# A hybrid encoder block: q and k of both halves projected before V, all turned by VectorE

## The chip, the cores and the metric

The kernel runs on one core of a Trainium2 chip. The metric is device time of one execution in microseconds (us). The kernel before takes 1110.05 us (median of 3 runs, 1109.37 to 1110.4). Engines are named as in the profile: PE (TensorE's matmuls), PEld (its weight loads), DVE (VectorE), ACT (ScalarE), POOL (GpSimd), SP (SyncE, here only a queue that issues transfers).

## The reference

One layer on x of 512 tokens by 1024 features, all in float32: a half-step feed-forward block, then a mixer with two branches, then a second half-step feed-forward block. The tokens are an 8 x 64 grid; attention looks at a window of 8 rows by 16 columns.

```python
x = x + 0.5 * swiglu_1(rmsnorm(x))
h = rmsnorm(x)
xr, gr, q, k, v, ga, gb = split(h @ w_in)          # 7 parts of 1024 columns
xc = dwconv4(xr)                                   # then forward and backward RG-LRU
y_lru = (rglru_fwd(xc) + rglru_bwd(xc)) * gelu(gr)
q = rmsnorm_per_head(q) * 64 ** -0.5               # 16 heads of 64
k = rmsnorm_per_head(k)
s = q . k over the 8 x 16 window + bias[head, drow, dcol]
y_att = softmax(s) @ v
x = x + (sigmoid(ga) * y_lru + sigmoid(gb) * y_att) @ w_out
x = x + 0.5 * swiglu_2(rmsnorm(x))
```

## The kernel before

Every matmul is made of three passes: each float32 operand is split into a high and a low part (ACT writes the high part, line 145, DVE the low one, line 148), and PE adds high x low, high x high and low x high. A weight tile of 128x1024 (512 KB) comes by SP's queue into `wraw` (3 buffers) and is split into `wh` and `wl` (4 buffers each); PE uses such a tile, a chunk here, for 24 matmuls of 512 columns.

The stage that matters runs from about 358 to 700 us. First come eight chunks for the LRU's x (`wxr`), then the projections of q, k and V, each in two halves of 512 columns (8 heads). One half of one projection is a group: four chunks, four PSUM tiles `acc` by tokens (`tok_group`, lines 834 to 836). Then come 24 chunks of gates (`wg`), and the output projection.

Beside these groups the rest of the mixer is woven in by hand. It is written as Python generators, the lanes: `lru`, `att`, `tail`, `v` and `prep`. After each piece of PE work `weave` lets every lane go on by as many steps as the table RATE gives for the present phase (the phases here: xr, t0, t1, g). The program so written is then ordered for each engine by a scheduler: an engine's instructions, and the transfers that SP issues, run strictly in the order that comes out, and each waits for what it needs. `hold` ties an instruction behind PE's last projection matmul.

The groups come in the order q, k, V of the first half, then q, k, V of the second. q and k (`qk_raw`) are evicted by ACT to `qk` tiles with tokens on the partitions (line 846), squared and summed. They have to be normed and turned so that features lie on the partitions:

- First half: `norm_qk` scales them (line 912), and in `heads`, tile by tile (four feature tiles of two heads each), `start` has PE turn them against an identity, 4 + 4 matmuls of 128x128 (lines 949 and 951), into auxiliary PSUM. From there ACT and DVE make the high and low parts `qh`, `ql`, `kh`, `kl`.
- Second half: DVE turns them in blocks of 32x32 (line 916), SP stores them to DRAM (`qd`), and `fetch` brings one feature tile back, in pieces of 256 bytes, into `xqk` (one buffer), the next tile when `start` has read the last.

V is evicted by DVE (line 859), stored to DRAM by SP (`vd`, line 863) and read back by POOL in shifted forms (`vs`, `va`, `ve`).

Attention then goes in units. `scores` is 12 matmuls (line 988) per unit in the first half (8 units), 24 in the second (4 units); DVE adds the bias and takes the maximum (line 1008), ACT exponentiates and scales (lines 1015 and 1020); `ship` turns the weights on DVE (lines 1029 and 1030), stores them by SP (`pd`) and reads them back by POOL into `PT`. `apply` multiplies them by V (line 1051), ATT_LAG units later.

The lane `lru` does the gated recurrence by LRU_PLAN: small gate matmuls on PE (line 742), ACT's functions, DVE's scans (lines 787 and 789).

Of the kernel before, what the change touches and what calls it, by code (L numbers as in the profile page):

```python
# [9 lines left out]
F32 = mybir.dt.float32  # L10
# [6 lines left out]
P = 128  # L17
T = 512
# [45 lines left out]
ATT_LAG = 4, 2  # L64
# [20 lines left out]
    "t0": {"att": 0.0, "lru": 3.25},  # L85
    "t1": {"att": 0.75, "tail": 0.75, "lru": 2, "prep": 1.0},
    "g": {"att": 0.7, "tail": 0.7, "lru": 1.5, "v": 0.5, "prep": 1.0},
# [4 lines left out]
def block_kernel(ctx: ExitStack, tc, a, out):  # L92
# [616 lines left out]
    def lru():  # L709
# [17 lines left out]
        def cut(f):  # L727
            cuts[f] = tuple(big.tile([P, T], F32R, tag="PT", bufs=5, name=nm(n)) for n in ("ch", "cl"))
            split(xc[f], *cuts[f])
# [32 lines left out]
        def use(f, d):  # L762
            r, ix = got[f, d]
            hold(nc.vector.tensor_tensor(ix, ix, xc[f], ALU.mult))
            if d == 1 and f < 3:
                th = big.tile([P, T], F32, name=nm("th"), **(dict(tag="xqk", bufs=1) if f == 0 else dict(tag="PT", bufs=5)))
            else:
                th = big_t(n="th")
            act("tanh", nc.scalar.activation(th, r, AF.Tanh, scale=sp4[:, f * 2 + d : f * 2 + d + 1]))
            got[f, d] = r, ix, th  # L770
# [128 lines left out]
    def norm_qk(raws, st, qd):  # L899

        rq = tiny.tile([P, 2, NCB, 8], F32, tag="rq", name=nm("rq"))
        for w in range(2):
            for j in range(NCB):
                hold(nc.vector.tensor_scalar(rq[:, w, j, :], st[:, w, j, :], 1.0 / HD, epsv[:, j : j + 1],
                                             ALU.mult, ALU.add))
        hold(nc.scalar.activation(rq, rq, AF.Sqrt))
        nc.vector.reciprocal(rq, rq)
        yield
        for j in range(NCB):
            for w in range(2):  # L910
                t = raws[w][j].rearrange("p (h d) -> p h d", d=HD)
                hold(nc.vector.tensor_tensor(t, t, rq[:, w, j, :].unsqueeze(2).to_broadcast([P, 8, HD]), ALU.mult))
            if qd is not None:
                t2 = pair_t().rearrange("p a b -> p (a b)")
                for w in range(2):
                    nc.vector.transpose(
                        t2.rearrange("p (c f w i) -> p w f c i", c=NCB, f=4, w=2)[:, w],
                        raws[w][j].rearrange("p (f c i) -> p f c i", c=NCB, i=32))
                nc.sync.dma_start(qd[j], t2)
                yield  # L920
            elif j % 2 == 1:
                yield
        if qd is not None:
            yield
            fetch(qd, 0)

    xs = {}

    def fetch(qd, fi):
        t = xs[fi] = big.tile([P, NCB * NCB, 2, 32], F32, tag="xqk", bufs=1, name=nm("xqk"))  # L930
        for c in range(NCB):
            nc.sync.dma_start(
                t[c * 32 : (c + 1) * 32].rearrange("p g w i -> p g (w i)"),
                qd.rearrange("j (a i) c f x -> c f i (j a) x", a=NCB)[c, fi])

    def heads(hf, raws, qd):

        if hf == 1:
            until("prep", lambda: False)
# [3 lines left out]
        def start(fi):  # L943
            rev = lambda t: t.rearrange("p (j t) -> p j t", j=NCB)[:, :, ::-1]
            if hf == 0:
                fs = slice(fi * P, (fi + 1) * P)
                pq, pk = aux_t(), aux_t()
                for j in range(NCB):
                    hold(nc.tensor.transpose(pq[:, j * P : (j + 1) * P], raws[0][j][:, fs], ident))
                for j in range(NCB):  # L950
                    hold(nc.tensor.transpose(perm(pk)[:, j], raws[1][j][:, fs], ident))
                xq, xk = pq.rearrange("p (j t) -> p j t", j=NCB), pk
                q_of, k_of = rev, lambda t: t
            else:
                x = xs.pop(fi).rearrange("p (j a) w i -> p w j a i", j=NCB)
                xq, xk = x[:, 0], x[:, 1].rearrange("p j a (r c) -> p j a r c", r=2)
                q_of = lambda t: rev(t).rearrange("p j (a i) -> p j a i", i=32)
                k_of = lambda t: t.rearrange("p (a r j c) -> p j a r c", a=NCB, r=2, j=NCB)
# [7 lines left out]
            if hf == 1 and fi < 3:  # L966
                fetch(qd, fi + 1)
# [55 lines left out]
        def ship(fi, n2):  # L1023
# [9 lines left out]
            PT = big.tile([P, NCB, 7, 32], F32, tag="PT", bufs=5, name=nm("PT"))  # L1033
# [65 lines left out]
    bias(0)  # L1099
    for hf in range(2):  # L1100
        st = tiny.tile([P, 2, NCB, 8], F32, tag="st", name=nm("st"))
        raws = [qk_raw(0, hf, st), qk_raw(1, hf, st)]
        if hf == 1:
            qd = dram.tile([NCB, P, NCB, 4, 64], F32, name="qd")
            lanes["prep"].append(norm_qk(raws, st, qd))
        v_get(hf)
        if hf == 0:
            lanes["att"].append(norm_qk(raws, st, None))
        lanes["att"].append(heads(hf, raws, qd if hf == 1 else None))
        phase[0] = "t1" if hf == 0 else "g"  # L1110

# [145 lines left out]
```

## Time and profile before

| | |
|---|---|
| median of 3 runs | 1110.05 us |
| the profiled execution, in whole | 1108.49 us |
| its span on the core | 1106.7 us |
| PE busy in the span | 1093.7 us, 99% |
| granted PE clock | 1.0 throughout |
| bytes moved | 180 MB, 163 GB/s on average |

A page counts an engine as busy from an instruction's start to its end. PE's matmuls are pipelined and overlap, so what a matmul costs in a row of equal ones is the distance of the starts, not its duration. The views that the prediction uses are the busy time of each engine in stretches of 50 us, the groups of instructions by line and tile, the waits (who waited, for what, how long in total, how often, longest), the chain of work that ended last in order of time, and single instructions in order of time. Times in them count from the start of the span.

### The profile page before, as it was taken

The numbers are of one execution on the slowest core, as the hardware profiler recorded it, in microseconds if no ns is written. First come the engines' busy times: TensorE is split into PE (matmuls) and PEld (weight loads), VectorE is DVE, ScalarE is ACT, GpSimd is POOL, SyncE is SP. The second block draws the span as 40 slices with busy tenths as digits, with TensorE's granted clock in tenths as the row PEclk, the third lists the DMA queues.
The fourth block names the chain that finished last, engine by engine and source line by source line (L and its number), as shares of the span: only waits on it lengthen the run. The fifth ranks groups of instructions, "written<-read, shape, count | busy, mean of one in ns | idle before, by whom it ended". The sixth has DMA issues, their size and how long they took to land.

```text
span 1106.7 us, 17673 instructions
## 1 busy us (share of the span) xinstructions
PE 1093.7 (99%) x6779; PEld 969.0 (88%) x6779; DVE 796.1 (72%) x1228; ACT 619.1 (56%) x950; POOL 140.1 (13%) x243
## 2 busy tenths in 40 slices
PE   9999999999999999999999899999999999999998
PEld 7899999988888778787877778889999999998887
DVE  7877777795745786998886664659877777784642
ACT  8554544464443668777778673456655454464430
POOL 0000000000000342231325430001000000000000
PEclk9999999999999999999999999999999999999999
DMA  8576656643423576573799973477665666653421
GB/s 268 153 172 153 148 158 160 165 153 96 134 81 105 163 231 172 157 225 111 222 281 256 270 219 97 131 227 163 184 164 149 165 166 146 151 167 96 133 76 39
DMA packets 68452, 180.02 MB, mean 163 GB/s; under 512 B 17681, under 2 KB 21265, under 8 KB 68369
## 3 DMA queue, kind: packets, MB, share of 16 engines
q1 hardware_dynamic: 52160, 131.94, 36.8%
q0 software_dynamic: 15632, 46.70, 21.5%
q8 instruction: 53, 0.87, 0.3%
q10 hardware_dynamic: 576, 0.26, 0.1%
q14 instruction: 31, 0.25, 0.1%
HBM read 152.63 MB, written 17.83 MB: 154 GB/s over the span
## 4 chain that ended last, share of the span: by engine, by line
PE 95%; DMA 1%; DVE 1%; ACT 1%; issue 1%; SPq 0%; ACTq 0%; DVEq 0%
PE acc L312 31%; PE acc L172 11%; PE acc L173 10%; PE acc L174 10%; PE aux L312 5%; PE acc L834 4%; PE aux L172 4%; PE aux L174 4%; PE aux L173 4%; PE acc L835 4%; PE acc L836 4%; PE aux L1051 1%; PE aux L742 1%; PE aux L988 1%; DMA vd<-v 1%
## 5 line engine op out<-in xcount | busy, mean ns | idle before, releaser
L145 ACT ACTIVATE wh<-wraw 128x1024 fp32r<-128x1024 f32 (+3 forms) x236 | 233.4, 991 | 321.6 <-issue 90.5
L148 DVE TENSOR_TENSOR wl<-wraw,wh 128x1024 fp32r<-128x1024 f32 (+3 forms) x236 | 267.6, 1137 | 99.5 <-ACT wh L145 95.9
L312 PE MATMUL acc<-s,wh 128*128 128x256 f32 x1280 | 232.2, 283 | 0.0
L312 PEld LDWEIGHTS acc<-s,wh 128*128 128x128 f32 x1280 | 199.7, 192 | 0.0
L312 PE MATMUL acc<-s,wl 128*128 128x256 f32 x640 | 181.2, 283 | 0.0
L312 PEld LDWEIGHTS acc<-s,wl 128*128 128x128 f32 x640 | 122.9, 192 | 0.0
L172 PE MATMUL acc<-xh,wh 128*128 128x512 f32 x272 | 107.7, 396 | 0.0
L174 PE MATMUL acc<-xh,wl 128*128 128x512 f32 x272 | 106.3, 391 | 0.0
L173 PE MATMUL acc<-xl,wh 128*128 128x512 f32 x272 | 106.0, 390 | 0.0
L312 PE MATMUL acc<-xl,wh 128*128 128x256 f32 x320 | 90.6, 283 | 0.0
L312 PE MATMUL acc<-xh,wl 128*128 128x256 f32 x320 | 90.6, 283 | 0.0
L312 PE MATMUL acc<-xh,wh 128*128 128x256 f32 x320 | 90.6, 283 | 0.0
L834 PE MATMUL acc<-wh,xh 128*128 128x512 f32 x192 | 75.7, 394 | 1.0 <-ACT qk L846 1.0
L148 DVE TENSOR_TENSOR hl<-h,hh 128x512 fp32r<-128x512 f32 x88 | 57.3, 687 | 25.4 <-PE aux L173 24.2
L835 PE MATMUL acc<-wh,xl 128*128 128x512 f32 x192 | 74.8, 390 | 0.0
L836 PE MATMUL acc<-wl,xh 128*128 128x512 f32 x192 | 74.8, 389 | 0.0
L172 PE MATMUL aux<-hh,wh 128*128 128x512 f32 (+1 forms) x181 | 69.9, 386 | 0.0
L173 PE MATMUL aux<-hl,wh 128*128 128x512 f32 (+1 forms) x181 | 69.9, 386 | 0.0
L174 PE MATMUL aux<-hh,wl 128*128 128x512 f32 (+1 forms) x181 | 69.9, 386 | 0.0
L174 PE MATMUL acc<-hh,wl 128*128 128x512 f32 (+1 forms) x176 | 68.0, 386 | 0.0
L173 PE MATMUL acc<-hl,wh 128*128 128x512 f32 (+1 forms) x176 | 68.0, 386 | 0.0
L172 PE MATMUL acc<-hh,wh 128*128 128x512 f32 (+1 forms) x176 | 67.9, 386 | 0.0
(226 smaller groups left out, 2281.8 us busy)
## 6 DMA issues: line engine op xcount, KB each, us to landing
wraw<-wqkv SPq DMA_DIRECT2D x24, 512.0 KB
wraw<-wg SPq DMA_DIRECT2D x24, 512.0 KB
wraw<-w1d SPq DMA_DIRECT2D x22, 512.0 KB
wraw<-w2s SPq DMA_DIRECT2D x22, 512.0 KB
pair<-w2s SPq DMA_DIRECT2D x22, 512.0 KB
wraw<-w2d SPq DMA_DIRECT2D x22, 512.0 KB
wraw<-w1s SPq DMA_DIRECT2D x18, 512.0 KB
pair<-w1s SPq DMA_DIRECT2D x18, 512.0 KB
```

The costliest lines, as they stand in the source:

```text
L145: nc.scalar.activation(H, raw, AF.Copy)
L148: return nc.vector.tensor_tensor(L, raw, H.bitcast(F32), ALU.subtract)
L172: nc.tensor.matmul(ps, wh, xh, start=first, stop=False, skip_group_check=skip)
L173: nc.tensor.matmul(ps, wh, xl, start=False, stop=False, skip_group_check=skip)
L174: mark["mm"] = nc.tensor.matmul(ps, wl, xh, start=False, stop=last, skip_group_check=skip)
L312: mm = nc.tensor.matmul(o, w_[:, c], x_, start=first and m + k == 0 and w_ is H and x_ is xh_, stop=m + k == 4 and w_ is L, skip_group_che ...
L742: prev, mm = mm, nc.tensor.matmul(ps[d][b], W[w][o, c], X[x][o], start=x == 1, stop=w + x == 0)
L834: nc.tensor.matmul(pss[j], xh[kk][:, tj], H[:, s], start=kk == 0, stop=False)
L835: nc.tensor.matmul(pss[j], xl[kk][:, tj], H[:, s], start=False, stop=False)
L836: mark["mm"] = nc.tensor.matmul(pss[j], xh[kk][:, tj], L[:, s], start=False, stop=kk == KT - 1)
L988: mm = hold(nc.tensor.matmul(ps[hp][:, cs], q_[o, n * P : (n + 1) * P], keys(k_[o]), start=k_ is kl, stop=q_ is ql))
L1051: mm = nc.tensor.matmul(pv[h2 * HD : (h2 + 1) * HD, n * P : (n + 1) * P], vt[:, (fi * 2 + h2) * HD : (fi * 2 + h2 + 1) * HD], PT[:, q], st ...
```

## The change

The order of the six groups becomes q, k of the first half, q, k of the second, V of the first, V of the second. `norm_qk` now turns both halves by DVE into a `qd` of its own for each half, in the lane `prep`, while the next group runs; `heads` no longer uses PE for it. `xqk` has two buffers, and two tiles are fetched ahead: tiles 0 and 1 by `norm_qk`, tiles 2 and 3 when `start` has read the tile two before. The fetches of the second half wait until tile 3 of the first half has been asked for. PT has 4 buffers instead of 5, and the LRU's `th` tiles use the two `xqk` buffers and PT. RATE has one more phase (t2), fewer LRU steps per call in most phases, and no attention before t2; the first half's value product comes 3 units after its scores instead of 4.

```diff
-ATT_LAG = 4, 2
+ATT_LAG = 3, 2
...
-    "t0": {"att": 0.0, "lru": 3.25},
-    "t1": {"att": 0.75, "tail": 0.75, "lru": 2, "prep": 1.0},
-    "g": {"att": 0.7, "tail": 0.7, "lru": 1.5, "v": 0.5, "prep": 1.0},
+    "t0": {"att": 0.0, "lru": 3},
+    "t1": {"att": 0.0, "lru": 2.5, "prep": 1.25},
+    "t2": {"att": 0.7, "tail": 0.7, "lru": 2, "prep": 1.0},
+    "g": {"att": 0.6, "tail": 0.6, "lru": 1.5, "v": 0.5, "prep": 1.0},
...
-            if d == 1 and f < 3:
-                th = big.tile([P, T], F32, name=nm("th"), **(dict(tag="xqk", bufs=1) if f == 0 else dict(tag="PT", bufs=5)))
+            if d == 1 and f < 4:
+                th = big.tile([P, T], F32, name=nm("th"), **(dict(tag="xqk", bufs=2) if f < 2 else dict(tag="PT", bufs=4)))
...
-    def norm_qk(raws, st, qd):
+    def norm_qk(hf, raws, st):
...
         for j in range(NCB):
+            t2 = pair_t().rearrange("p a b -> p (a b)")
             for w in range(2):
                 t = raws[w][j].rearrange("p (h d) -> p h d", d=HD)
                 hold(nc.vector.tensor_tensor(t, t, rq[:, w, j, :].unsqueeze(2).to_broadcast([P, 8, HD]), ALU.mult))
-            if qd is not None:
...
+                nc.vector.transpose(
+                    t2.rearrange("p (c f w i) -> p w f c i", c=NCB, f=4, w=2)[:, w],
+                    raws[w][j].rearrange("p (f c i) -> p f c i", c=NCB, i=32))
+            nc.sync.dma_start(qd[hf][j], t2)
             yield
-            fetch(qd, 0)
+        while hf == 1 and (0, 3) not in xs:
+            yield
+        for fi in range(2):
+            fetch(hf, fi)
...
-            if hf == 0:
-                fs = slice(fi * P, (fi + 1) * P)
-                pq, pk = aux_t(), aux_t()
-                for j in range(NCB):
-                    hold(nc.tensor.transpose(pq[:, j * P : (j + 1) * P], raws[0][j][:, fs], ident))
-                for j in range(NCB):
-                    hold(nc.tensor.transpose(perm(pk)[:, j], raws[1][j][:, fs], ident))
...
+            x = xs[hf, fi].rearrange("p (j a) w i -> p w j a i", j=NCB)
...
-            if hf == 1 and fi < 3:
-                fetch(qd, fi + 1)
+            if fi < 2:
+                fetch(hf, fi + 2)
...
+    def qk_half(hf):
+        st = tiny.tile([P, 2, NCB, 8], F32, tag="st", name=nm("st"))
+        raws = [qk_raw(0, hf, st)]
+        if hf == 1:
+            phase[0] = "t2"
+        raws.append(qk_raw(1, hf, st))
+        qd[hf] = dram.tile([NCB, P, NCB, 4, 64], F32, name=nm("qd"))
+        lanes["prep"].append(norm_qk(hf, raws, st))
+        lanes["att"].append(heads(hf))
+
     for hf in range(2):
...
+        qk_half(hf)
+        phase[0] = ("t1", "t2")[hf]
+    for hf in range(2):
         v_get(hf)
...
+    phase[0] = "g"
```

Three places of the order that the scheduler makes. The first is PE's, at the first tile of the first half: before, in the third chunk of the second half's k group, `aux` taking the turned `qk` tiles.

```order
L836 MATMUL acc_5123<-wl_5159,xh_3092 128x512
...
L836 MATMUL acc_5123<-wl_5159,xh_3094 128x512
L949 MATMUL aux_5187<-ident,qk_4441 128x128
L949 MATMUL aux_5187<-ident,qk_4443 128x128
L949 MATMUL aux_5187<-ident,qk_4445 128x128
L949 MATMUL aux_5187<-ident,qk_4447 128x128
L951 MATMUL aux_5188<-ident,qk_4626 128x8x16
L951 MATMUL aux_5188<-ident,qk_4628 128x8x16
L951 MATMUL aux_5188<-ident,qk_4630 128x8x16
L951 MATMUL aux_5188<-ident,qk_4632 128x8x16
L834 MATMUL acc_5120<-wh_5208,xh_3096 128x512
```

The same place now, after the same number of rows on PE: the middle of the first half's V group (lines are one higher in this part, ten lower further down).

```order
L836 MATMUL acc_5122<-wh_5182,xl_3095 128x512
L837 MATMUL acc_5122<-wl_5183,xh_3094 128x512
L978 MATMUL aux_5213<-kl_5156,qh_5153 128x256
L978 MATMUL aux_5212<-kl_5156,qh_5153 128x256
L978 MATMUL aux_5213<-kh_5155,qh_5153 128x256
L978 MATMUL aux_5212<-kh_5155,qh_5153 128x256
```

The turns are gone, and the scores of the first unit stand at this point; the next unit's follow two chunks later, at the end of the group.

The second place is SP's queue around the stores of the first half's V (`vd`). Before, weights of the next group (`wraw_5124`, `wraw_5157`) are asked for ahead of these stores; the loads of the second half's V group, `wraw_5403` and `wraw_5444`, stand a few rows behind them, a whole group ahead of their use.

```order
L163 DMA wraw_5124<-wqkv 128x1024
L163 DMA wraw_5157<-wqkv 128x1024
L863 DMA vd_81<-v_4881 8x16x512
L863 DMA vd_81<-v_4883 8x16x512
L863 DMA vd_81<-v_4885 8x16x512
L863 DMA vd_81<-v_4887 8x16x512
L163 DMA wraw_5207<-wqkv 128x1024
L163 DMA wraw_5304<-wqkv 128x1024
L163 DMA wraw_5403<-wqkv 128x1024
L163 DMA wraw_5444<-wqkv 128x1024
```

Now: `xqk_5161` and `xqk_5264` are tiles 2 and 3 of the first half, `pd_5249` the weights of the first unit, `qd_5118` the turned q and k of the second half, and `wraw_5449` and `wraw_5542` the first two loads of the second half's V group, which is the very next group on PE.

```order
L930 DMA xqk_5161<-qd_4661 32x16x64 x4
L1022 DMA pd_5249<-pt_5246 128x896
L930 DMA xqk_5264<-qd_4661 32x16x64 x4
L918 DMA qd_5118<-pair_5281 128x1024
L918 DMA qd_5118<-pair_5320 128x1024
L864 DMA vd_81<-v_5356 8x16x512
L864 DMA vd_81<-v_5358 8x16x512
L864 DMA vd_81<-v_5360 8x16x512
L864 DMA vd_81<-v_5362 8x16x512
L918 DMA qd_5118<-pair_5439 128x1024
L164 DMA wraw_5449<-wqkv 128x1024
L164 DMA wraw_5542<-wqkv 128x1024
```

All of the second V group's loads stand behind the stores of the first V group and behind stores and fetches of q and k; no later load has been moved ahead of them.

The third place is DVE's order between the last evictions of the first half's V and the low part `wl_5451` of that first load.

```order
L860 TENSOR_SCALAR v_5362<-acc_5122,rcol_3719 128x512
L794 TENSOR_TENSOR th_5018<-th_5018,th_5023 128x512
L915 STREAM_TRANSPOSE pair_5320<-qk_4898 128x4x4x32
L914 TENSOR_TENSOR qk_5094<-qk_5094,rq_5170 128x512
L788 SCALAR_TENSOR_TENSOR th_5113<-gate_4843,gate_4844 128x512
L915 STREAM_TRANSPOSE pair_5320<-qk_5094 128x4x4x32
L790 SCALAR_TENSOR_TENSOR th_5116<-gate_4852,gate_4853 128x512
L914 TENSOR_TENSOR qk_4900<-qk_4900,rq_5170 128x512
L794 TENSOR_TENSOR th_5113<-th_5113,th_5116 128x512
L915 STREAM_TRANSPOSE pair_5439<-qk_4900 128x4x4x32
L914 TENSOR_TENSOR qk_5096<-qk_5096,rq_5170 128x512
L915 STREAM_TRANSPOSE pair_5439<-qk_5096 128x4x4x32
```

Scans of the LRU and turns of the second half's q and k stand here, where before the evictions of the second V group were followed by that of a gate's weight; the row behind the last one is the split of `wraw_5449` itself.

More of the change, by code (lines that the diff above doesn't have):

```diff
@@ L727, in cut @@
         def cut(f):
-            cuts[f] = tuple(big.tile([P, T], F32R, tag="PT", bufs=5, name=nm(n)) for n in ("ch", "cl"))
+            cuts[f] = tuple(big.tile([P, T], F32R, tag="PT", bufs=4, name=nm(n)) for n in ("ch", "cl"))
             split(xc[f], *cuts[f])
@@ L912, in norm_qk, with fetch @@
                 hold(nc.vector.tensor_tensor(t, t, rq[:, w, j, :].unsqueeze(2).to_broadcast([P, 8, HD]), ALU.mult))
-            if qd is not None:
[L914 to L923, printed above, removed]
-            yield
-            fetch(qd, 0)
-    xs = {}
-    def fetch(qd, fi):
-        t = xs[fi] = big.tile([P, NCB * NCB, 2, 32], F32, tag="xqk", bufs=1, name=nm("xqk"))
+                nc.vector.transpose(
+                    t2.rearrange("p (c f w i) -> p w f c i", c=NCB, f=4, w=2)[:, w],
+                    raws[w][j].rearrange("p (f c i) -> p f c i", c=NCB, i=32))
+            nc.sync.dma_start(qd[hf][j], t2)
+            yield
+        while hf == 1 and (0, 3) not in xs:
+            yield
+        for fi in range(2):
+            fetch(hf, fi)
+    qd, xs = {}, {}
+    def fetch(hf, fi):
+        t = xs[hf, fi] = big.tile([P, NCB * NCB, 2, 32], F32, tag="xqk", bufs=2, name=nm("xqk"))
         for c in range(NCB):
@@ L933, in fetch, with heads @@
                 t[c * 32 : (c + 1) * 32].rearrange("p g w i -> p g (w i)"),
[L934 to L939, printed above, removed]
+                qd[hf].rearrange("j (a i) c f x -> c f i (j a) x", a=NCB)[c, fi])
+    def heads(hf):
+        until("prep", lambda: (hf, 0) in xs)
+        if hf == 0:
+            yield
+            yield
         qk, rss, soft, PTs = {}, {}, {}, {}
@@ L944, in start @@
             rev = lambda t: t.rearrange("p (j t) -> p j t", j=NCB)[:, :, ::-1]
-            if hf == 0:
-                fs = slice(fi * P, (fi + 1) * P)
-                pq, pk = aux_t(), aux_t()
-                for j in range(NCB):
-                    hold(nc.tensor.transpose(pq[:, j * P : (j + 1) * P], raws[0][j][:, fs], ident))
-                for j in range(NCB):
[L951 to L958, printed above, removed]
+            x = xs[hf, fi].rearrange("p (j a) w i -> p w j a i", j=NCB)
+            xq, xk = x[:, 0], x[:, 1].rearrange("p j a (r c) -> p j a r c", r=2)
+            q_of = lambda t: rev(t).rearrange("p j (a i) -> p j a i", i=32)
+            k_of = lambda t: t.rearrange("p (a r j c) -> p j a r c", a=NCB, r=2, j=NCB)
             qh, ql, kh, kl = (big_t(F32R, n=n) for n in ("qh", "ql", "kh", "kl"))
@@ L1032, in ship @@
             nc.sync.dma_start(d, t.rearrange("p c q i -> p c (q i)"))
-            PT = big.tile([P, NCB, 7, 32], F32, tag="PT", bufs=5, name=nm("PT"))
+            PT = big.tile([P, NCB, 7, 32], F32, tag="PT", bufs=4, name=nm("PT"))
             for c in range(4):
@@ L1099, in block_kernel @@
     bias(0)
-    for hf in range(2):
[L1101 to L1105, printed above, removed]
+    def qk_half(hf):
[7 more added lines that the diff above has]
+        lanes["att"].append(heads(hf))
+    for hf in range(2):
+        qk_half(hf)
+        phase[0] = ("t1", "t2")[hf]
+    for hf in range(2):
         v_get(hf)
[L1107 to L1110, printed above, removed]
+    phase[0] = "g"
     def gates(w, fs, fn, scale=1.0):
```

## The prediction

> **What bounds the kernel now.** I read the page's busy shares first, then the busy time by stretch, then the waits, then single instructions in order of time.
>
> ```profile
> span 1106.7 us, 17673 instructions
> PE 1093.7 (99%) x6779; PEld 969.0 (88%) x6779; DVE 796.1 (72%) x1228; ACT 619.1 (56%) x950; POOL 140.1 (13%) x243
> ...
> 450.00:500.00 50.00, 50.00 (x230) 40.39 (x229) 47.80 (x68) 39.64 (x54) 18.06 (x31) 1.00 0.70 196
> 500.00:550.00 50.00, 49.03 (x259) 39.67 (x259) 43.13 (x97) 37.73 (x81) 10.62 (x19) 1.00 0.53 163
> 550.00:600.00 50.00, 48.74 (x311) 39.89 (x312) 38.43 (x99) 38.88 (x83) 17.26 (x29) 1.00 0.96 275
> 600.00:650.00 50.00, 44.27 (x313) 36.58 (x313) 35.21 (x89) 36.49 (x85) 24.05 (x41) 1.00 0.92 257
> ```
>
> TensorE (PE) is the bound: the time can only fall by taking work off it or by filling the places where it waits. Columns of a stretch are its length, then busy time of PE, weight load, VectorE (DVE), ScalarE (ACT), GpSimd, then clock, DMA share and GB/s. In 500 to 650 us, the stage that the change rewrites, PE idles 0.97 + 1.26 + 5.73 = 8.0 us. Note also that VectorE, in 450 to 500, is busy 47.8 of 50 us: the new turns have little room there.
>
> ```profile
> PE aux L988 <- DVE kl L965: 5.7, 3, 2.8
> PE aux L1051 <- DVE ql L962: 1.3, 1, 1.3
> ...
> PE acc L834 <- ACT qk L846: 1.0, 1, 1.0
> ```
>
> These waits are the 8 us: three times the scores (L988) of the second half wait for `kl`, the low part of k, once a value product and once a projection wait for what VectorE or ScalarE still does for q and k of the first half.
>
> **What goes.** PE's turns of the first half:
>
> ```profile
> 508.46 0.39 PE L835 MATMUL acc<-wh,xl 128*128 128x512 f32 x1
> 508.68 0.40 PE L836 MATMUL acc<-wl,xh 128*128 128x512 f32 x1
> 508.92 0.60 PE L949 MATMUL aux<-ident,qk 128*128 128x128 f32 x4
> 509.36 0.60 PE L951 MATMUL aux<-ident,qk 128*128 128x128 f32 x4
> 509.71 0.48 PE L834 MATMUL acc<-wh,xh 128*128 128x512 f32 x1
> ```
>
> Ends overlap, so starts count: from L836 to the next L834 1.03 us pass, where 0.23 separates neighbours without turns. Eight turns cost 0.80 us, four feature tiles **3.2 us**, all on the path. One weight chunk of 24 such matmuls is 24 x 0.228 = 5.5 us.
>
> Of the 8.0 us of waits I take back **5.0**. The two of the first half (2.2) hang on auxiliary PSUM and on ScalarE's evictions at the step from k to V, both of which the change moves. Of the three of the second half (5.7) the fetch two tiles ahead removes what the transfer causes, but the new order still has VectorE evict a gate chunk (L1113) just ahead of `kl` of that half's first tile, as before at
>
> ```profile
> 607.86 0.24 PE acc L174
> ...
> 608.73 0.69 DVE kl L965
> 609.56 1.00 PE aux L988 x12
> ```
>
> where PE stands 1.5 us from L174's end (608.10) to the scores. I keep that one and 1.5 for the rest. Bounds: 2.0 to 8.0 taken back.
>
> **What is added, off the path.** VectorE gets eight more 128x512 turns, 8 x 0.69 = 5.5 us, and DMA another 2 MB out and in. LRU work, ring sizes (PT, xqk) and the later V shuffle I cost at nothing: they lie beside PE's chunks, and the room of some 15 us between a score and its value product covers them; without that cover they would cost the 0 to 3 us that the upper end of the range holds.
>
> **What is moved: the loads of the second V group.** All weight loads and all traffic of q, k and V leave through SP's one queue, in order. Today V's loads stand early:
>
> ```profile
> 491.74 0.33 SPq L163 DMA_DIRECT2D wraw<-wqkv  x1
> ...
> 524.73 0.50 PE L834 MATMUL acc<-wh,xh 128*128 128x512 f32 x1 [0.97 <-ACT qk L846]
> ```
>
> This is the first load of the second V group and its first matmul: 33 us of lead. In the new order that load stands behind a fetch that needs `kl` of tile 0, the store of the first unit's weights, a fetch that needs `kl` of tile 1, two stores of turned q and k, four stores of the first V group, and a third store of turned q and k (the SP rows in the section on the change). What each of them waits for is ready only around the end of the first V group or after it, and the queue stands meanwhile:
>
> ```profile
> SPq L163 <- DVE wl L148: 399.0, 100, 7.2
> ...
> SPq L863 <- DVE v L859: 4.5, 3, 2.7
> ...
> SPq L919 <- DVE pair L916: 3.4, 2, 2.6
> ```
>
> SP spends 399 us of this run waiting for a buffer at its head, and did wait for V and for turned tiles when these stood there. So I work out when the last store ahead of the load can leave. PE issues as many rows before the first scores as it did before the turns at 508.92, so it reaches them at 508.9; scores of a unit take 0.94 us and 0.2 of switching:
>
> ```profile
> 515.41 0.94 PE aux L988 x12
> ```
>
> Two chunks later, at 508.9 + 1.1 + 10.9 = 521.0, the first V group ends; after the second unit's scores, at **522.2**, PE wants the second V group. VectorE then does, from the first V eviction to the turn that the last store ships, 4 evictions, 4 scans, 2 additions, 3 multiplications and 4 turns:
>
> ```profile
> L787 DVE TENSOR_TENSOR_SCAN th<-gate,gate 128x512 f32<-128x512 f32 x8 | 9.7, 1214 | 0.0
> L859 DVE TENSOR_SCALAR v<-acc,rcol 128x512 f32<-128x512 f32 x8 | 5.7, 746 | 0.1
> L793 DVE TENSOR_TENSOR th<-th,th 128x512 f32<-128x512 f32 x8 | 5.5, 685 | 0.1
> L916 DVE STREAM_TRANSPOSE pair<-qk 128x512 f32<-128x512 f32 x8 | 5.3, 688 | 0.0
> ...
> 564.74 1.27 DVE L916 STREAM_TRANSPOSE pair<-qk 128x512 f32<-128x512 f32 x2
> 565.93 1.26 DVE L912 TENSOR_TENSOR qk<-qk,rq 128x512 f32<-128x512 f32 x2
> ```
>
> Back to back each takes 0.08 less than its duration (two turns in 1.19 from start to start), so 4 x 0.67 + 4 x 1.13 + 9 x 0.605 = 12.6 us; after the last eviction 8.3 of them remain, its own included. If VectorE is never late, the load leaves at 521.0 + 8.3 = 529.3. It will be late. Up to `kl` of tile 0 the new order gives it, from the point that both orders share (the split of the ninth projection weight, first row below), 12 weight splits and 12 scans at 1.13 to 1.14, 59 operations on 128x512 at 0.60 and some short ones of 3.4 together, 66 us,
>
> ```profile
> 441.08 1.23 DVE L148 TENSOR_TENSOR wl<-wraw,wh 128x1024 fp32r<-128x1024 f32 x1 [1.62 <-ACT wh L145]
> ...
> 453.18 1.27 DVE L851 TENSOR_REDUCE st<-sq 128x8 f32<-128x512 f32 x2
> ...
> 518.00 0.35 DVE L1008 CUSTOM_DVE_ANT_0 so<-aux,bm 128x192 f32<-128x192 f32 x1
> ...
> 522.39 0.57 DVE L1029 STREAM_TRANSPOSE pt<-p 128x384 f32<-128x384 f32 x1
> ```
>
> and 3 more since the sums of squares of k cannot come before 453, when they came here: 441 + 66 + 3, `kl` at 510, the first scores at 511 instead of 508.9 (estimates). From a unit's first eviction to its turned weights 4.4 us pass (518.00 to 522.39); with `ql`, `kl`, two turns and some LRU work the V evictions begin at 522, and the load leaves at 522 + 12.6 + 0.4 = **535**. Its landing is bounded by a quiet load, issued at 500.35 and over by 504, 3.2 to 3.6 us,
>
> ```profile
> 500.35 0.33 SPq L163 DMA_DIRECT2D wraw<-wqkv  x1
> ...
> 503.00:504.00 1.00, 1.00 (x6) 0.82 (x5) 1.00 (x3) 1.00 (x3) 0.00 (x0) 1.00 0.95 290
> 504.00:505.00 1.00, 1.00 (x6) 0.84 (x5) 1.00 (x3) 1.00 (x2) 0.00 (x0) 1.00 0.08 21
> ...
> 548.63 6.40 DMA vd<-v
> ...
> L148 DVE TENSOR_TENSOR wl<-wraw,wh 128x1024 fp32r<-128x1024 f32 x59 | 72.0, 1220 | 16.3 <-ACT wh L145 13.4 <-PE aux L742 2.5
> L145 ACT ACTIVATE wh<-wraw 128x1024 fp32r<-128x1024 f32 x59 | 62.4, 1058 | 67.4 <-PE acc L173 36.2 <-PE acc L835 20.3 <-issue 9.2
> ```
>
> and by 6.4 us for V's stores, which run at the same moment; I take the middle, 4.8. Then come 1.06 for `wh` and 1.22 for `wl`, of which PE hides 0.5 behind its first two matmuls: PE goes on at 541.5, **19.3 us late**, the 2 us at the first scores included. Best: 529.3 + 3.2 + 1.8 = 534.3, 12.1 late. Worst: VectorE 4 us later and 6.4 for the landing, 547.2, 25 late. The two next loads leave right behind and arrive within PE's chunk of 5.5 us. In the wait VectorE and ScalarE stand too, since their next rows are this weight's split.
>
> **Sum.** -3.2 - 5.0 + 19.3 = +11.1 us. The profiled execution took 1108.5 us (its span and 1.8 around it), 1.6 less than the median 1110.05; I add the sum to the median: **1121 us**. Ends: -3.2 - 8.0 + 12.1 = +0.9, and -3.2 - 2.0 + 25 = +19.8: 1111 to 1130.
>
> **Rivals.** (1) The stores ahead of the load cost only their issue, 16 of them at 0.33 to 0.6 us, some 7 us; the load then leaves near 500, lands long before 522, and the kernel is faster: -3.2 - 5.0, 1102 (1099 to 1105). It decides from where the load leaves before 524, since 8.2 us late is break-even. Against it stand the 399 us of waits at the head of SP. [...] Chance 0.10. (2) The wait is there, but near its lower end, and most idle time comes back: 1108 to 1112, no change; for it speaks that VectorE had 2.2 us to spare in 450 to 500. Chance 0.10. (3) The change does not do what it says: `kl` of the second half stays late by VectorE's order, 2 us taken back, or V's shuffle is late for the first product: 1124 to 1130, inside the forecast's upper half, with 0.2 of its chance. Forecast, with (3): 0.80, of which 0.05 lies above 1130.
>
> **How the numbers follow.** About 0.2% (2.2 us) is what a measurement of this kernel can tell from no change. Slower by more has 0.80, within it 0.10, faster 0.10. The range 1110 to 1130 leaves out rival 1, part of rival 2 and the tail above.
>
> **What would show it.** Right: the turns (L949, L951) gone from PE, one idle stretch of PE of 10 to 20 us at the start of the second V group, released by a weight's split, with SP's load issued after V's stores; `kl` no longer among PE's waits but once or twice. Wrong: V's loads issued before 524, or PE stopping elsewhere in the stage, above all at the first scores, where a slow fetch of q and k would make the 2 us more.

## The result, and the profile after

The changed kernel takes **1127.72 us** (median of 4 runs), the kernel before, run beside it, 1110.22 us. The ratio is 1.0156, with a 95% interval of 1.0132 to 1.0179: slower by 17.5 us. The forecast was 1121 us in a range of 1110 to 1130. Medians here and below count every execution; one of the four of product_later, a run below, was slow (1183.26 us at a mean clock of 0.851) and is left out of its ratio, and its median without it is 1100.37 us.

| | before | after |
|---|---|---|
| median, us | 1110.22 | 1127.72 |
| profiled execution, us (its span) | 1108.49 (1106.7) | 1128.83 (1127.0) |
| PE busy, us (share) | 1093.7 (99%) | 1095.4 (97%) |
| PE idle in 450 to 700 us | 8.0 | 27.0 |
| granted clock, mean | 1.000 | 0.988 |

The page of the changed kernel: the head, and the one group of PE that waits long (after the bar, busy time, mean ns, and the idle time just before the group with what ended most of it).

```profile
span 1127.0 us, 17607 instructions
PE 1095.4 (97%) x6747; PEld 968.5 (86%) x6747; DVE 801.2 (71%) x1236; ACT 616.4 (55%) x948; POOL 140.1 (12%) x243
...
L835 PE MATMUL acc<-wh,xh 128*128 128x512 f32 x192 | 77.7, 405 | 24.6 <-ACT wh L146 22.1
```

Its busy time by stretch, same columns as in the prediction:

```profile
450.00:500.00 50.00, 47.52 (x211) 37.76 (x210) 49.88 (x74) 39.83 (x57) 8.26 (x16) 0.97 0.65 191
500.00:550.00 50.00, 27.84 (x133) 22.02 (x132) 33.58 (x64) 19.47 (x37) 6.85 (x11) 0.80 0.49 141
550.00:600.00 50.00, 49.07 (x289) 39.16 (x288) 33.03 (x91) 34.79 (x87) 21.55 (x35) 0.96 0.93 266
600.00:650.00 50.00, 48.62 (x300) 39.71 (x299) 35.56 (x84) 38.28 (x76) 24.10 (x39) 1.00 0.90 251
```

Most of the loss lies in one stretch, 500 to 550, and there in one wait. The instructions around it, in order of time (start, duration, engine, line; in brackets the idle time before and what ended it):

```profile
521.58 0.74 DVE L860 TENSOR_SCALAR v<-acc,rcol 128x512 f32<-128x512 f32 x1
...
530.71 3.68 SPq L864 DMA_DIRECT2D vd<-v  x4
...
533.82 0.71 DVE L915 STREAM_TRANSPOSE pair<-qk 128x512 f32<-128x512 f32 x1
...
535.74 4.43 SPq L164 DMA_DIRECT2D wraw<-wqkv  x3
...
547.09 1.06 ACT L146 ACTIVATE wh<-wraw 128x1024 fp32r<-128x1024 f32 x1 [26.50 <-DMA wraw<-wqkv]
548.18 1.23 DVE L149 TENSOR_TENSOR wl<-wraw,wh 128x1024 fp32r<-128x1024 f32 x1 [13.65 <-ACT wh L146]
...
548.20 0.79 PE L835 MATMUL acc<-wh,xh 128*128 128x512 f32 x1 [22.12 <-ACT wh L146]
```

This is the picture that the prediction drew: four stores of V, the third store of turned q and k, and only then, at 535.74, the first load of the second V group. ScalarE stood 26.5 us for it and PE 22.1.

Two more things cost time that no term had foreseen. The granted clock is half in and behind the wait:

```profile
540.00:550.00 10.00, 1.76 (x3) 1.00 (x4) 1.23 (x1) 1.89 (x2) 3.38 (x5) 0.50 0.90 247
550.00:555.00 5.00, 5.00 (x14) 3.88 (x13) 4.26 (x12) 3.63 (x9) 2.64 (x4) 0.56 0.83 243
555.00:560.00 5.00, 5.00 (x30) 3.83 (x30) 4.11 (x10) 3.64 (x12) 2.15 (x4) 1.00 0.79 249
```

From 548.20 to 554.32 there are 13 matmul starts, 6.1 us, where 13 x 0.228 = 3.0 is the usual pace: 3.2 us (from exact starts). And at 476 PE waits for ScalarE's eviction of a finished q group; these are the waits of the changed kernel in 470 to 560 (engine, line, what ended the wait: total, times, longest):

```profile
PE acc L835 <- ACT wh L146: 22.1, 1, 22.1
...
PE acc L835 <- ACT qk L847: 2.5, 1, 2.5
```

ScalarE had, ahead of that eviction, four sigmoids and two exponentials of LRU units, two table loads and three splits, 9.2 us from 468.7 on. Half clock followed this wait too: 13 matmuls start in 479 to 483, where two runs below with the same wait kept the full clock and have 20 (loads_ahead) and 18 (stores_by_pool). That is 1.6 us.

The account, in the profiled executions:

| | us |
|---|---|
| PE's turns gone (L949, L951 are no longer on PE) | -3.2 |
| waits in 500 to 700: 8.0 before, 0.93 + 1.38 left beside the one below | -5.7 |
| eviction at 476, 2.5 idle and 1.6 at half clock | +4.1 |
| first weight of the second V group | +22.1 |
| half clock behind it | +3.2 |
| sum | +20.5 |
| measured, 1128.83 - 1108.49 | +20.3 |

The medians differ by 17.5 us and not by 20.3, since the profiled execution of before was 1.7 us under its median and that of the changed kernel 1.1 over.

So far the prediction's mechanism is what the trace shows. Whether that load is also the *cause* of the loss, in that the time comes back when it is on time, only runs can tell.

### The profile page after: what moved, and what is told of

Read it like the earlier page. It is cut to its first block, busy times and chain, and to the rows that moved or that the text cites. A ratio compares the mean times of both kernels' runs of the same rounds, so it can differ in the third digit from the quotient of the medians.

```text
span 1127.0 us, 17607 instructions
## 1 busy us (share of the span) xinstructions
PE 1095.4 (97%) x6747; PEld 968.5 (86%) x6747; DVE 801.2 (71%) x1236; ACT 616.4 (55%) x948; POOL 140.1 (12%) x243
## 4 chain that ended last, share of the span: by engine, by line
PE 93%; DMA 2%; issue 2%; POOL 1%; DVE 1%; ACT 1%; SPq 0%; ACTq 0%; POOLq 0%
PE acc L313 31%; PE acc L173 11%; PE acc L174 10%; PE acc L175 10%; PE aux L313 5%; PE aux L173 4%; PE aux L174 4%; PE aux L175 4%; PE acc L835 3%; PE acc L836 3%; PE acc L837 3%; PE aux L1041 1%; PE aux L743 1%; DMA PT<-pd 1%; PE aux L978 1%
## 5 line engine op out<-in xcount | busy, mean ns | idle before, releaser
L835 PE MATMUL acc<-wh,xh 128*128 128x512 f32 x192 | 77.7, 405 | 24.6 <-ACT wh L146 22.1
```

The lines of the kernel that those rows point to most:

```text
L835: nc.tensor.matmul(pss[j], xh[kk][:, tj], H[:, s], start=kk == 0, stop=False)
```

## The experiments

Times are medians; the ratio is to the kernel before on the same chip (1109.1 to 1109.4), with its 95% interval. Times in a text are the run's own.

| run | order of groups | us | ratio |
|---|---|---|---|
| loads_ahead | q k q k V V | 1133.79 | 1.0223 (1.0205 to 1.0241) |
| stores_by_pool | q k q k V V | 1125.14 | 1.0145 (1.0124 to 1.0167) |
| old_order_new_turns | q k V q k V | 1129.54 | 1.0178 (1.016 to 1.0195) |
| new_order_old_turns | q k q k V V | 1125.28 | 1.0145 (1.0119 to 1.0171) |
| loads_by_act | q k q k V V | 1138.44 | 1.0269 (1.0253 to 1.0284) |
| old_order_loads_by_act | q k V q k V | 1111.65 | 1.0017 (1.0008 to 1.0027) |
| before_loads_by_act | q k V q k V | 1112.53 | 1.003 (1.0017 to 1.0043) |
| scores_after_v | q k q k V V | 1125.03 | 1.0142 (1.0127 to 1.0157) |
| product_later | q k V q k V | 1100.92 | 0.9916 (0.9896 to 0.9935) |
| product_later_lru_earlier | q k V q k V | 1098.52 | 0.991 (0.9884 to 0.9937) |
| new_order_both_mends | q k q k V V | 1145.42 | 1.0337 (1.0316 to 1.0358) |
| v_before_k_both_mends | q k q V k V | 1114.31 | 1.005 (1.0035 to 1.0065) |

### Is it the place of the load?

**loads_ahead**: the second V group's loads get a higher priority.

```diff
-        ld = nc.sync.dma_start(raw[:, s], src[:, s])
+        with tc.high_priority() if early else nullcontext():
+            ld = nc.sync.dma_start(raw[:, s], src[:, s])
...
-            H, L = load_w(a["wqkv"][w * 2 + hf, kp], 1024)
+            H, L = load_w(a["wqkv"][w * 2 + hf, kp], 1024, early=w == 2 and hf == 1)
```

> Changed kernel, but the four weight loads of the second V group have a higher priority, so SP's queue takes three of them between the fetches of the first q/k tile and the fourth in the next tile's, ahead of all stores of V and of turned q and k of the second half; VectorE's order then has their low parts ahead of the V evictions. Theory (PE stood because the load left SP at 535.7): the idle stretch of 22.3 us at the start of the second V group goes, and with it the 3.2 us of half clock behind it; the 4.4 us at 475.7 (PE behind ScalarE's eviction) stay: 1127.7 - 25.5 = 1102. Rival (VectorE is overfull with the turns, so the low part of the weight is late in any place): PE still stands 8 to 12 us there or at the first scores, 1110 to 1116.

Neither: 1133.79, *slower* than the changed kernel. The loads did leave early and the 22.1 us went down to 3.2. These are the waits of this run in 500 to 640:

```profile
ACT wh L146 <- DMA wraw<-wg: 24.9, 3, 21.9
...
PE aux L978 <- DVE kl L955: 14.5, 2, 7.8
...
PE aux L1041 <- DMA PT<-pd: 4.0, 1, 4.0
...
PE acc L835 <- DVE v L860: 3.2, 1, 3.2
```

PE's waits sum to 22.4 us again, in five pieces (one of 0.7 us is not shown). What became late is read on SP and ScalarE:

```profile
529.95 4.75 SPq L864 DMA_DIRECT2D vd<-v  x4
...
539.95 2.32 SPq L165 DMA_DIRECT2D wraw<-wg  x3
...
547.42 1.06 ACT L146 ACTIVATE wh<-wraw 128x1024 fp32r<-128x1024 f32 x1 [21.90 <-DMA wraw<-wg]
```

The first weight behind the stores is now one of the gates, and it too is split at 547. This time ScalarE stands for it with the softmax of the first half queued behind, and that softmax makes `kl` and the scores late. The late weight was handed on, not removed. That the run is slower than the changed kernel with no more waits comes from the clock: PE works on at half clock behind most of these pieces (granted 0.83 in 550 to 600 and 0.93 in 600 to 650, for 0.96 and 1.00 in the changed kernel). Estimated as half of PE's busy time under half clock, this costs 8.8 us here and 4.8 us there.

**stores_by_pool**: instead, the stores leave SP's queue.

```diff
-            nc.sync.dma_start(qd[hf][j], t2)
+            (nc.gpsimd if hf == 1 else nc.sync).dma_start(qd[hf][j], t2)
...
-            nc.sync.dma_start(vd[hf][:, j * QC : (j + 1) * QC, :], V[hf, 2 * j])
+            (nc.gpsimd if hf == 0 else nc.sync).dma_start(vd[hf][:, j * QC : (j + 1) * QC, :], V[hf, 2 * j])
```

> Changed kernel, but the stores of the second half's turned q and k and of the first V group leave through GpSimd's queue; loads stay where the order has them, now with no store but the first unit's weights ahead of them, and VectorE's row for the low part of the first load stays behind the turns. Theory: the load leaves SP at about 524 (behind the fetch of tile 3) and lands by 530; the low part follows VectorE's last turn at 534.5, PE goes on at about 535.5: idle 9 to 10 us instead of 22.3, still with half clock behind it, 1114 to 1117. Rival (the transfer itself is slow, 10 us or more whenever V is moved): PE goes on after 540, 1120 or more. Rival (VectorE bounds it): same as the theory, and then a load that is earlier still cannot help without a new VectorE order.

1125.14: the rival's time, but not by the rival's mechanism. The load left SP at 522.58, and the loads of that moment took 7.2 us in the median. ScalarE came to it late:

```profile
533.73 0.51 ACT L1005 ACTIVATE p<-so,nmx 128x256 f32<-128x256 f32 x1 [14.26 <-DVE nmx L998]
...
537.43 1.99 ACT L146 ACTIVATE wh<-wraw 128x1024 fp32r<-128x1024 f32 x2
```

It stood 14.3 us at a softmax row whose maximum VectorE gives only behind its turns; PE waited 13.6 us and went on at 538.5, so the theory's 9 to 10 us were missed as well. A load that leaves early does not help while the split stands late in another engine's order.

### Which half of the change?

**old_order_new_turns** moves V back; **new_order_old_turns** keeps the new order and lets PE turn the first half again (rates, lag and rings as in the changed kernel).

```diff
     for hf in range(2):
         qk_half(hf)
         phase[0] = ("t1", "t2")[hf]
-    for hf in range(2):
         v_get(hf)
```

> Changed kernel, but the groups in the order of before (q, k, V of a half, then of the other); all turns on VectorE, two tiles ahead. In SP's order the loads of the second V group then stand ahead of the stores. Theory (only the place of the loads costs): no idle stretch over 3 us, 1127.7 - 25.5 = 1102, give or take 3. Rival (the turns and the second trip through DRAM cost by themselves, VectorE being busy 49.9 of 50 us): 1110 or more even in this order.

```diff
-                nc.vector.transpose(
+                hf and nc.vector.transpose(
...
-            nc.sync.dma_start(qd[hf][j], t2)
+            hf and nc.sync.dma_start(qd[hf][j], t2)
...
+            if hf == 0:
+                for j in range(NCB):
+                    hold(nc.tensor.transpose(pq[:, j * P : (j + 1) * P], raws[0][j][:, fs], ident))
+                for j in range(NCB):
+                    hold(nc.tensor.transpose(perm(pk)[:, j], raws[1][j][:, fs], ident))
```

> Changed kernel with the new order of groups, but the first half's q and k turned by PE as before (no turned store and no fetch for it). In SP's order the loads of the second V group then stand ahead of all stores. Theory (only the place of the loads costs): no idle stretch over 3 us at the start of the second V group; 1127.7 - 25.5 + 3.2 for PE's turns = 1105, give or take 3. Rival (the order of the groups costs by itself, V being shuffled a group later): PE waits 10 us or more for V or for weights in it, 1115 or more.

Both rivals' times come in: each half of the change, with the changed kernel's rates, lag and rings, costs about as much as both, 1129.54 and 1125.28. Their reasons do not hold as they stand, and the two lose in different places. In the old order it is not VectorE or its turns that PE waits for; PE stops among the gates, and this is the chain of waits there:

```profile
570.43 12.43 DMA PT<-pd
...
583.11 1.98 PE aux L1041 x16
...
606.17 0.34 SPq L1022
606.56 5.47 DMA wraw<-wg
612.05 1.06 ACT wh L146
613.16 0.79 PE acc L173
```

Again a weight behind a store (L1022, the weights of an attention unit, ready at 606), 14.8 us of PE. In the new order with PE's turns no weight is late; its chain in 545 to 570:

```profile
557.64 1.53 POOL va L884 x2
...
559.96 6.57 DMA bm<-rpb
566.66 0.36 DVE so L1010
...
567.52 1.08 PE aux L951 x4
```

`va` and `ve` are the shuffle of the first half's V through GpSimd's queue; `bm` is the bias that a score row needs. The shuffle stands ahead of the bias in that queue, VectorE waits for the bias, and PE 5.3 us for the PSUM tile that VectorE has not emptied; another 3.8 us of PE end with `kl`. PE's order is also cut up finer: in 440 to 720 it changes 59 times between chunks, LRU gates, turns, scores and products, where the kernel before changes 43 times, some 1.7 us by the starts of its instructions.

### A queue of their own for the weights

```diff
-        ld = nc.sync.dma_start(raw[:, s], src[:, s])
+        ld = (nc.scalar if own else nc.sync).dma_start(raw[:, s], src[:, s])
...
-            H, L = load_w(a["wqkv"][w * 2 + hf, kp], 1024)
+            H, L = load_w(a["wqkv"][w * 2 + hf, kp], 1024, own=w == 2 and hf == 1)
...
-            feat_chunk(a["wg3"][w * KT + f], KT, xh, xl, ps, 0, KT, True, RATE[phase[0]])
+            feat_chunk(a["wg3"][w * KT + f], KT, xh, xl, ps, 0, KT, True, RATE[phase[0]], True)
```

> Changed kernel, but the weight loads of the second V group and of all gate chunks leave through ScalarE's queue, so no weight stands behind a store or a fetch of q, k or V any more; SP keeps stores and fetches. Theory now (in the changed kernel any weight behind those stores comes at about 547, whichever it is: moving four loads ahead only made the next group's first weight the late one, and ScalarE stood 21.9 us for it): no wait of PE that ends with a weight, and the softmax of the first half no longer behind one. What is left is V: its first group ends at 521 to 525, its shuffle at about 564, so the first value product waits until 565 to 572 where PE would be there at 554: 1110 to 1118. Rival (the DMA engines are full there, so everything comes late whatever the queue): waits of PE sum to 20 us or more as before, 1122 or more. Rival (loads are all that matters): no wait over 3 us, 1102.

> The kernel with the order of groups of before and all turns on VectorE, two tiles ahead (1129.54 with its loads in SP's queue, PE 15 us behind a gate weight that stood behind a store and 9 us at a value product whose weights landed 12 us after their issue), with the weight loads of the second V group and of the gates on ScalarE's queue. V is stored a group earlier here, so its shuffle is done before the first value product. Theory: the 15 us go, with the half clock behind them (3 us); the value product's own wait is partly the crowd of stores and loads let go at once, 3 to 9 us remain: 1103 to 1112. Rival (full DMA engines): the weight still lands late, 1120 or more.

> Control: the kernel before, with the weight loads of the second V group and of the gates on ScalarE's queue. Theory: its loads were never late (its 8 us of waits end with kl, ql and an eviction), so within 3 us of before, 1107 to 1113. If ScalarE's time for issuing loads, or its standing at them, costs by itself, it shows here as more than 1113, and has to be taken off the other two.

In the **old order** the theory holds: 1111.65, 17.9 us less than with the loads on SP, and in the control, 1112.53, the move alone costs some 3 us. No wait of PE over 2.1 us ends with a weight any more; the first value product is still late, by 8.6 us of idle time, and this chain of waits says why:

```profile
571.84 1.67 POOL PT L1026 x3
573.51 9.58 DMA PT<-pd
...
583.34 0.69 PE aux L1041 x4
```

Its weights (`PT`) take 9.6 us to land, in a stretch (560 to 590) where the DMA engines are 97 to 102% busy.

In the **new order** the theory fell: 1138.44. The rival's figures come in (1122 or more, and PE's waits in 500 to 640 sum to 28 us), but not its reason, since none of these waits ends with a weight. With the loads on time, ScalarE's splits stand ahead of the softmax and wait for PE to free a weight buffer:

```profile
532.85 1.06 ACT L146 ACTIVATE wh<-wraw 128x1024 fp32r<-128x1024 f32 x1 [4.51 <-PE acc L836]
...
550.35 1.06 ACT L146 ACTIVATE wh<-wraw 128x1024 fp32r<-128x1024 f32 x1 [4.38 <-PE acc L836]
...
554.35 0.51 ACT L1005 ACTIVATE p<-so,nmx 128x256 f32<-128x256 f32 x1
```

`kl` is made behind that softmax, and PE waits 14.5 us for it in all. Here PE also waits for V's shuffle itself:

```profile
PE aux L1041 <- DMA va<-vd: 5.4, 1, 5.4
```

### Scores behind V

```diff
-    "t2": {"att": 0.7, "tail": 0.7, "lru": 2, "prep": 1.0},
+    "t2": {"att": 0.0, "tail": 0.7, "lru": 2, "prep": 1.0},
```

> Changed kernel with one number changed: the attention lane takes no step (rate 0.0 for 0.7) during the groups from the second half's k on, so the first scores stand behind the second V group instead of in the middle of the first. Same order of groups, same turns, loads in SP's queue; they now stand beside stores that wait for nothing but V itself, not behind fetches and unit weights. Theory (in the new order the first half's softmax, its biases and its unit weights go through the same queues as V's stores and V's shuffle, at the same moment; each in-order queue then has something unready at its head, and which of weights, biases or kl comes late is chance): waits of PE fall under 10 us in all, 1104 to 1113. Rival (the order itself leaves too little work for PE beside the attention, or VectorE is the bound): 1120 or more, with the waits further down among the gates.

1125.03, so only the first half of the theory holds: from 450 to 700 us PE's waits sum to 9.4 us, none over 5; but the attention now ends late, and from 701 on PE stands 11.0 us for `kl` of the last tile, while ScalarE is still at the softmax of the tile before. The gain is given back at the end. Time and place are the rival's (1120 or more, among the gates); which of its two reasons holds is not shown.

### A later value product

In the old order with loads by ScalarE:

```diff
-ATT_LAG = 3, 2
+ATT_LAG = 4, 2
...
-    NBIG = 41
+    NBIG = 39
...
-            PT = big.tile([P, NCB, 7, 32], F32, tag="PT", bufs=4, name=nm("PT"))
+            PT = big.tile([P, NCB, 7, 32], F32, tag="PT", bufs=5, name=nm("PT"))
```

> Order of groups of before, all turns on VectorE, loads of the second V group and the gates on ScalarE's queue (1111.65), and the value product one unit later (lag 4 instead of 3, with a fifth PT buffer, for which two of the 41 general tiles are given up). Theory: PE's 8.8 us before the first value product (PT landed 9.6 us after its issue, the DMA engines being full) is covered by one more unit of scores and some 36 matmuls of a gate: 1102 to 1106, faster than both kernels. Rival (full DMA engines only move the wait to the next thing fetched): 1109 or more.

```diff
-    "t0": {"att": 0.0, "lru": 3},
+    "t0": {"att": 0.0, "lru": 3.25},
```

> As the run before it, and the LRU lane takes 3.25 steps a call in the first phase as in the kernel before, instead of 3. In the changed kernel PE waits 2.6 us at 475.7 for ScalarE's eviction, behind the sigmoids of an LRU unit and two table loads, with half clock behind it in some runs (1.6 us). Theory: with the old rate the unit falls a chunk earlier and this wait goes: 2 to 4 us less than the run before, 1099 to 1103. Rival: the wait moves to another eviction: within 1 us of the run before.

Both are **faster than both kernels, 1100.92 and 1098.52**, 1.1 and 0.5 us under the ranges of their theories. The intervals of the two overlap, so the last 2.4 us are not told apart by the times; the trace shows the wait at 476 gone, which was 2.1 us in product_later (there it ended with ScalarE's split of a weight). The faster one by stretch:

```profile
450.00:500.00 50.00, 50.00 (x230) 40.35 (x229) 49.93 (x73) 37.86 (x52) 14.56 (x26) 1.00 0.72 225
500.00:550.00 50.00, 50.00 (x243) 40.62 (x242) 44.73 (x87) 30.29 (x57) 6.92 (x10) 1.00 0.63 170
550.00:600.00 50.00, 48.23 (x264) 38.92 (x263) 33.87 (x78) 38.30 (x74) 19.77 (x33) 1.00 1.03 284
```

PE idles 1.8 us in 450 to 700 where the kernel before idles 8.0, at full clock. VectorE is as full in 450 to 500 as in the changed kernel (49.93 of 50), so the turns need not hold PE up.

### The same mends in the new order

> Changed kernel (new order: q, k, q, k, V, V) with the two mends that made the old order fast: weight loads of the second V group and of the gates on ScalarE's queue, value product one unit later (lag 4, five PT buffers, 39 general tiles). In the old order the two took the time from 1129.5 to 1100.9. Theory (besides late loads the new order has a cost of its own: the first half's V is stored only at 521 to 527, while its scores run from 513 on, so V's shuffle, the biases and the unit weights meet in GpSimd's queue): PE still waits 15 us or more between 525 and 630, 1118 or more. Rival (late loads and the early value product are all there is): 1099 to 1106, as in the old order.

The third order differs from it in two places:

```diff
         if hf == 1:
+            v_get(0)
             phase[0] = "t2"
...
-    for hf in range(2):
-        v_get(hf)
+    v_get(1)
```

> The same with the first half's V a group earlier (order q, k, q, V, k, V), so it ends near 498 and its shuffle is done before the first scores, which the order then puts in the last group. Theory (the distance from V to its use is what the new order lacks): 1099 to 1106, as in the order of before. Rival (q and k of the second half ahead of V cost by their own turns and stores): 1115 or more.

This pair says most about where the new order's cost lies. With the mends that bring the old order to 1100.92, the new order takes 1145.42, the slowest of all; with V of the first half one group earlier 31.1 us of that come back. The pair moves two things, though: V is evicted from 500.6 on instead of 526.8, and the first scores start at 541.0 instead of 513.1. So it shows that V and the scores must lie further apart, not which of the two has to move. (In scores_after_v the scores moved without these mends, for 1125.03.) GpSimd, VectorE and ScalarE in the slow one:

```profile
548.78 0.63 POOL L873 DMA_DIRECT2D vs<-vd  x1 [13.46 <-DMA vd<-v]
...
573.31 1.69 POOL L896 DMA_DIRECT2D bm<-rpb  x3
574.99 3.84 POOL L1026 DMA_DIRECT2D PT<-pd  x7
...
576.62 0.36 DVE L998 CUSTOM_DVE_ANT_0 so<-aux,bm 128x192 f32<-128x192 f32 x1 [9.87 <-DMA bm<-rpb]
...
577.02 0.46 ACT L1005 ACTIVATE p<-so,nmx 128x192 f32<-128x192 f32 x1 [12.11 <-DVE nmx L998]
```

From the first read of V at 548.8 to 573.3 GpSimd's queue issues nothing but the shuffle; three biases and seven gathers of `PT` leave behind it; VectorE stands 9.9 us for a bias, and ScalarE 12.1 us for the maximum that needs it. But PE's idle time right behind this, at 574 and 580, is only 4.6 of its 35.3 us. Its longest waits are 6.0, 10.5 and 6.1 us, all for `kl`; this is the one of 10.5:

```profile
618.67 1.06 ACT L146 ACTIVATE wh<-wraw 128x1024 fp32r<-128x1024 f32 x1 [3.42 <-PE acc L174]
...
621.04 0.45 ACT L1005 ACTIVATE p<-so,nmx 128x192 f32<-128x192 f32 x1
...
631.30 0.58 PE L978 MATMUL aux<-kl,qh 64*128 64x256 f32 x2 [10.54 <-DVE kl L955]
```

It is the same picture as in loads_by_act: a split that waits for PE's buffer stands ahead of the softmax, and `kl` comes behind that. The 1114.31 of the other order lies between the theory's range and the rival's bound: two waits of 3.9 us remain beside the one of 2.5 at 476, for evictions by ScalarE (523) and VectorE (554), with half clock behind them (granted 0.93 on average in 500 to 550 and in 550 to 600). Why they come is open.

## Why the prediction was right, and where its reasons were not

**The time was right, 6.7 us above the forecast and inside the range; the step that it put all the loss on is seen in the trace, but is not by itself the cause.**

| step, as predicted | measured |
|---|---|
| PE's turns gone, -3.2 | gone |
| 5.0 of 8.0 us of waits taken back; the one behind L1113 stays with 1.5 | 5.7; 1.4 in 600 to 650, at the scores (L978 at 623) |
| `kl` at 510, first scores at 511 | `kl` at 509.1, scores at 513.0: PE itself was late, from the eviction at 476 |
| V's evictions from 522, 12.6 us on VectorE to the last turn | from 521.6, 13.0 us |
| load leaves SP at 535 | 535.74 |
| landing 4.8 us, bounds 3.2 to 6.4 | split begins 11.4 us after the issue |
| no term for the eviction at 476 | 2.5 us |
| no term for the clock | 3.2 + 1.6 us |
| one idle stretch of PE of 10 to 20 us | 22.1 us |
| PE goes on at 541.5 | 548.2 |

- **The queue.** The order of SP, the work that VectorE does ahead of the last store, and the moment of the issue were right to within a microsecond. Some luck is in the last: the first scores came 2 us later than predicted, behind the eviction at 476 and its half clock and with `kl` in time, and VectorE's work from there to V's evictions took 8.5 us instead of 11.
- **The mis-sized term is the landing.** It was bounded by a quiet load and by V's stores alone. The load shares the DMA engines with 1 MB of V's stores, 0.5 MB of turned q and k, two more loads right behind it and the shuffle's reads: 0.90 busy in 540 to 550. A better bound was the sum of what is in flight. As an estimate, these are some 4.2 MB, which at the 205 to 247 GB/s of 530 to 550 take 17 to 20 us from the first store at 530.7 on, to 548 to 551; the three loads were split at 547.1, 549.2 and 551.5.
- **The clock** had no term: 3.2 us behind the long wait, 1.6 behind the short one. All in all the account comes to +20.5 us in the profiled executions where the sum had +11.1. That the time still fell inside the range is owed to its width: its upper end was made of VectorE 4 us later, a landing of 6.4 us and only 2.0 us of waits taken back, and of these the landing alone came, and larger.
- **The step that failed** is the one that costed "LRU work, ring sizes (PT, xqk) and the later V shuffle" at nothing, with "0 to 3 us" without cover. In the changed kernel the first product waits only 0.9 us, for `PT` behind the shuffle (PE at 578), and PE had stood 22 us before. With the load of the second V group issued early the new order loses about as much (1125.1, 1125.3) or more (1133.8, 1138.4, 1145.4), now at biases, softmax, `kl` and products, and what brings time back is V further ahead of the scores (1114.3). The prediction's rival (3) named V's shuffle, at 1124 to 1130, and gave it a part of 0.2.
- **Rival (1)** said that the kernel is faster from where the load leaves before 524. In stores_by_pool it left at 522.6, and the time was 1125: the break-even was worked out for one queue, and ScalarE's and VectorE's orders stood behind it. The queue in which a load stands matters here, and not always for the better: the same loads through another engine's queue moved the time by -17.9 us in one order (1129.54 to 1111.65) and by +10.7 in the other (1127.72 to 1138.44).
- **The parts that were sound in the change** are the turns on VectorE and the fetch two tiles ahead: in the old order, with weights that no store holds up and with the lag of before, they give 0.9916 and 0.991. In the control ScalarE's queue cost 3 us; whether it costs that here is not shown. With the lag of 3 the first product waits 8.6 us there; in product_later the lag, a PT buffer and two general tiles changed together, and were not tried apart.

What stays open: the shuffle alone was not put on another queue in the new order, so its share beside the finer cut of PE's order (some 1.7 us in new_order_old_turns) and ScalarE's splits ahead of the softmax is not separated. Nor is V's place separated from the scores' in the last pair.

## What to carry to other kernels

A wait that ends the idle time of the bound engine is only the last of those that would have held it: before counting it as gain, ask what the engine meets next if it goes on at once, and price that from where the data was produced (here V, stored at 531, its shuffle issued until 565). A fixed order on several in-order queues is fragile where one producer is moved nearer to its consumer: whatever stands behind the first thing that is not ready comes late, and moving one victim makes the next (here the second V group's first weight, split at 547.1, and with that one moved ahead the gates', split at 547.4). Keep loads that depend on nothing out of queues that hold stores of fresh results, and leave distance between a result that must go through DRAM and its use. Here it took both: the loads' own queue brought 17.9 us where V lay far from its use, and cost 10.7 where it did not.

## What was not expected of the hardware

- **The clock falls after short waits, but not after each.** The same wait of 2.5 us at 476 was followed by half clock in the changed kernel and not in loads_ahead, here in the stretch behind it, the changed kernel first. The third row is old_order_new_turns, where the wait was 2.1 us:

```profile
479.00:483.00 4.00, 4.00 (x13) 3.10 (x12) 4.00 (x7) 4.00 (x8) 0.00 (x0) 0.57 1.00 298
```

```profile
479.00:483.00 4.00, 4.00 (x20) 3.24 (x19) 4.00 (x7) 4.00 (x8) 0.00 (x0) 1.00 0.95 300
```

```profile
479.00:483.00 4.00, 4.00 (x12) 3.09 (x11) 4.00 (x7) 2.25 (x3) 0.00 (x0) 0.59 1.02 308
```

  Behind the wait of 2.5 us the clock falls also in new_order_old_turns (0.97 on average over 480 to 520) and in new_order_both_mends (0.97 over 450 to 500, as in the changed kernel); it does not in stores_by_pool (1.00 in 479 to 483) and in v_before_k_both_mends (1.00 over 450 to 500). Nor does it behind the wait of 2.1 us in product_later (1.00 in 479 to 483), or behind one of 2.8 us at 628 in the kernel before (1.00 in every microsecond from 624 to 640). So 2.1 us were enough in one run and 2.8 us were not in another; what decides it is not shown.
- **Issuing a transfer can itself take long**: three loads took 4.43 us on SP at 535.74, the first of them 2.41, right behind the stores of V, and a single one 0.33 at 500.35 of the kernel before. That it comes from what is in flight is not shown: in loads_ahead three loads behind the same stores took 2.32 us.
